# T3 of the second phase's weights formed once and kept in HBM, its splits placed behind evictions, and another order of loads, evictions and normalizations in a Winograd kernel

## The chip, the cores and the metric

The kernel runs on one core of one Trainium2 chip. The metric is device time in microseconds (us) of one execution. Engines go by their names in the profile: PE (TensorE, matmuls), PEld (its weight loads), DVE (VectorE), ACT (ScalarE), POOL (GpSimd), SP (SyncE, here only the queue that issues most transfers). Each engine works through its own instructions in order; a DMA issue is an instruction too, and holds up what stands behind it on the engine that issues it.

## The reference, cut to what matters

With `DEPTH = 1` only the pooling layer runs. `x` is 4096 tokens by 1024 channels, all float32.

```python
normed = rms_norm(x, norm_w[0])
u, gate = jnp.split(normed @ in_w, 2, axis=-1)          # in_w: 1024 x 2048
ug = u.reshape(b, s, 4, 256)
pooled = stack([trailing_mean(ug[:, :, g], (2, 4, 8, 16)[g]) for g in range(4)]) - ug
mixed = einsum('bsgc,gcd->bsgd', pooled, group_w) + group_b
y = mixed.reshape(b, s, 1024) * scale * silu(gate)
h = x + y @ out_w                                        # out_w: 1024 x 1024
return rms_norm(h, final_norm_w)
```

Pooling is linear along the tokens, so the kernel multiplies `group_w` into the u columns of `in_w` first ("folding") and pools afterwards.

## The kernel before, in words

**Products.** The big matrix products are done by the Winograd scheme: seven products P1 to P7 of half-size blocks for eight. One operand block is split in four quarters 11, 12, 21, 22; the weights too. For the weights of the input projection, 11 and 21 are the upper and lower rows of a gate half of `in_w`, times `norm_w` (`norm_c`), and 12 and 22 are folded u weights. The products use the weights 11 (P1), 21 (P2), T2 = 11 + T3 (P6), T3 = 22 - 12 (P7), T1 = 22 - T2 (P5), T4 = 21 - T2 (P4) and 22 (P3).

**Precision.** Each factor is split in a rounded high part (a copy on ACT into fp32r, L151, or L218 with a scale) and the rest (a subtraction on DVE, L145, or L219), and a product is three matmuls: high by high, high by low, low by high (`mm3`, L529). A product of the input projection is 48 matmuls of 128x128x512 (`product_in`, L538).

**Steps.** `steps` (L851) is the order of the work: 28 steps "a" (four blocks of 1024 tokens, each P1, P2, P6, P7, P5, P4, P3, the first half of the columns), then 28 steps "b" (the second half, "the second phase"), then 56 steps "o" (output projection). They are numbered from 0 here, so step 5 is P4 of the first block, 7, 14 and 21 are P1 of the blocks after it, and step 30 is P6 of the first block of phase two. A step needs both parts of two operand tiles `op` (four tiles in a ring, two for each step) and both parts of its weight tiles `w`. P1 and P2 add up in banks 0 to 3: before P2 starts there, ACT copies P1's sums to banks 4 to 7 (L151 `bank<-bank`, in `evict_in`, L639).

**The main loop** (L1074) issues for step n: loads for step n + 3 or so; squares of the next block's rows (ACT, L381), from which the factors 1/rms come (ACT sqrt L196, DVE reciprocal L200, POOL L197 to L206) and go by HBM (`rd`) to all partitions; the normalization of the operands of step n + 2 (`form`, DVE L148), then the splits of step n + 1 (`split_step`); pooling; the matmuls and evictions of step n (`run`); and late in "a", `make_wb` (L275), which makes the weights of phase two one step at a time, from loads that `load_wb` (L256) issued a step before. A scheduler then orders each engine's instructions by its own estimates; `issue_after` pins one behind another.

**Weights of phase two.** `make_wb` forms T3 from wvd pieces "12" and "22" (folded, kept in HBM) twice, for P6 and again for P7, for each of two halves h of the rows; P5's weights are formed as 11 - 12 and split with the sign turned (`split_negative`, L160).

**The opening** (L914 to L1014) folds in eight chunks (`fold`, L343: matmuls L348, evictions L359 on DVE or L363 on ACT), loads the rows of the first block (L374) and the gate rows `g0` and `g1` (L212), squares the rows, spreads 1/rms over the partitions with two matmuls (`spread_rs`, L398: `hl` on ACT and POOL, L407 on DVE, L415 on PE, then a copy on ACT), and makes the first operands and weights. Tiles come from the slot pools `st`, `vt`, `early` and `early5`, first freed first taken.

Of the kernel before, what the change touches and what calls it, by code (L numbers as in the profile page):

```python
# [60 lines left out]
def kernel(  # L61
# [82 lines left out]
    def sub(dst, a, b):  # L144
        return nc.vector.tensor_tensor(out=dst, in0=a, in1=b, op=ALU.subtract)  # L145
# [11 lines left out]

    latest_split = [None]

    def split_negative(dst, src):  # L160
        nc.scalar.activation(dst[:, 0], src, AF.Copy, scale=-1.0)
        nc.vector.scalar_tensor_tensor(
            out=dst[:, 1], in0=src, scalar=-1.0, in1=dst[:, 0].bitcast(F32),
            op0=ALU.mult, op1=ALU.subtract,
        )
# [6 lines left out]
    tails = const.tile([P, 2, 2, HIST], F32, name="tails")  # L172

    wvd = [dram.tile([P, 2, H], F32, name=f"wvd{k}") for k in range(4)]
    wod = {
        i: [dram.tile([P, 2, H], F32, name=f"wod{i}_{h}") for h in range(2)]
        for i in range(P1, P7 + 1)
# [63 lines left out]
    def pair(cs, h, kh):  # L241
        k = 4 * kh + 2 * h
        return cs[k : k + 2]
# [24 lines left out]
    def scaled(u, cs, other, op):  # L268

# [2 lines left out]
                out=u[:, j], in0=u[:, j], scalar=cs[j], in1=other[:, j], op0=ALU.mult, op1=op  # L272
            )

    def make_wb(i):  # L275

        for h in range(2):
            p = parts.pop((i, h))
            top, bottom = pair(norm_c, h, 0), pair(norm_c, h, 1)
            if i == P1:  # L280
                split_scaled(w[i][h], p["11"], top)
            elif i == P2:
                split_scaled(w[i][h], p["21"], bottom)
            elif i == P6:
                sub(p["12"], p["22"], p["12"])
                scaled(p["11"], top, p["12"], ALU.add)
                t2[h] = p.pop("11")
                split(w[i][h], t2[h])
            elif i == P7:
                sub(p["22"], p["22"], p["12"])  # L290
                split(w[i][h], p["22"])
            elif i == P5:
                scaled(p["11"], top, p["12"], ALU.subtract)
                split_negative(w[i][h], p["11"])
            elif i == P4:
                scaled(p["21"], bottom, t2[h], ALU.subtract)
                split(w[i][h], p["21"])
                give(t2.pop(h))
            else:
                split(w[i][h], p["22"])  # L300
            for u in p.values():
                give(u)

    def make_wo(h):
# [35 lines left out]
            )  # L340
        return r

    def fold(q, k, g, r, ps2, pool=None, on_vector=()):  # L343
# [12 lines left out]
        o = take(pool=pool)  # L356
        for kk in range(2):
            if kk in on_vector:
                nc.vector.tensor_scalar(  # L359
                    out=o[:, kk], in0=ps2[kk], scalar1=norm_c[k + kk], scalar2=None, op0=ALU.mult  # L360
                )
            else:
                nc.scalar.activation(o[:, kk], ps2[kk], AF.Copy, scale=norm_c[k + kk])  # L363
        return o
# [587 lines left out]
                g0.append(load_rows(in_w, 2 * hh, D))  # L952
    give(gw[0])
    load(1)
    g1 = [load_rows(in_w, 4 + 2 * h, D) for h in range(2)]
    for j in range(4):
        load_row(0, 1, j, early if j < 3 else None)
    load(2)

    def second_side(h):  # L960
# [7 lines left out]
        split(w[P6][h], g0[h])  # L968

    for n, (h, k) in enumerate(chunks):  # L970
        o = fold(1, k, gw[1], ru[1, k], banks[2 * (n % 2) : 2 * (n % 2) + 2], early5, (0,))
        stores.append((wvd[k // 2], o))
        if n == 0:
            for hh in range(2):
# [8 lines left out]
    second_side(1)  # L983
    form(1)
    split_step(1)
    for h in range(2):
        split_scaled(w[P2][h], g1[h], pair(norm_c, h, 1))
    for j in range(4):
        square_row(0, 1, j)
    with tc.high_priority():  # L990
        rs = stats(0, 1)

    def spread_second():
        with tc.high_priority():
# [79 lines left out]
    for n in range(2, len(steps)):  # L1074
# [108 lines left out]
```

## Time and profile before

| | us |
|---|---|
| median of 3 runs (967.61 to 970.01) | 967.83 |
| the execution that was profiled | 966.88 |
| its span, first to last instruction | 965.1 |
| PE busy | 950.2 (98%) |
| DVE busy | 733.4 (76%) |
| ACT busy | 451.7 (47%) |
| granted TensorE clock | 0.999 |

Busy time of PE is made of matmuls that overlap, with modelled ends: a run of matmuls is read by its start, its count and its length. Where a line says that PE was idle and names a releaser, the wait ended with that instruction.

### The profile page before, as it was taken

The page shows a single profiled execution, that of the slowest core. Times are in us where ns is not written, and L with a number is a line of the kernel's source. Part 1 is how long each engine was busy: PE and PEld are TensorE (multiplying, and loading weights), DVE is VectorE, ACT ScalarE, POOL GpSimd, SP SyncE. Part 2 cuts the span into 40 slices and gives each one's busy share as a digit, 9 for nine tenths or more (in the row PEclk, how much of TensorE's full clock was granted, in tenths as well). Part 3 has the DMA queues.
Part 4 walks back from the last instruction along what each step waited for, and adds up shares of the span by engine and source line. Part 5 has one row for each costly group of instructions (what it writes and reads, how often), then busy time and mean ns, then how long its engine had stood idle before and what let it go on. Part 6 is the DMA issues. An engine that isn't in the chain of part 4 may idle for free.

```text
span 965.1 us, 11084 instructions
## 1 busy us (share of the span) xinstructions
PE 950.2 (98%) x4184; PEld 784.7 (81%) x4184; DVE 733.4 (76%) x804; ACT 451.7 (47%) x679; POOL 49.3 (5%) x128
## 2 busy tenths in 40 slices
PE   9999999999999998999999999999999999999997
PEld 7777888888888887888888888888888888888885
DVE  2896993793796898596697599499977667577565
ACT  5868447347345455345444445553424424324333
POOL 0032100000000000000000000000101101001010
PEclk9999999999999999999999999999999999999999
DMA  9975865564556646015614733635646436356022
GB/s 341 380 285 158 307 218 180 210 237 138 204 209 223 240 162 236 7 44 210 247 44 153 259 128 119 235 135 194 239 154 217 149 136 220 113 191 213 27 88 88
DMA packets 67685, 177.01 MB, mean 183 GB/s; under 512 B 6704, under 2 KB 24240, under 8 KB 67632
## 3 DMA queue, kind: packets, MB, share of 16 engines
q1 hardware_dynamic: 61584, 156.11, 46.1%
q10 hardware_dynamic: 4320, 13.91, 3.6%
q0 software_dynamic: 1728, 6.29, 1.7%
q8 instruction: 33, 0.54, 0.2%
q14 instruction: 20, 0.16, 0.0%
HBM read 116.50 MB, written 59.78 MB: 183 GB/s over the span
## 4 chain that ended last, share of the span: by engine, by line
PE 76%; DVE 13%; DMA 6%; issue 2%; ACT 1%; POOL 1%; SPq 0%; ACTq 0%; DVEq 0%; POOLq 0%
PE bank L532 76%; DVE op L145 2%; DVE st L148 2%; DVE w L145 2%; DVE vt L142 2%; DMA rd<-rs 1%; DMA st<-in_x 1%; DMA st<-in_in_w 1%; DMA st<-rd 1%; DVE w L219 1%; DVE st L145 1%; DMA vt<-rd 1%; DMA vt<-sd 1%; DVE st L621 1%; DVE vt L145 1%
## 5 line engine op out<-in xcount | busy, mean ns | idle before, releaser
L532 PE MATMUL bank<-op,w 128*128 128x512 f32 x2688 | 612.2, 390 | 5.6 <-DVE op L145 5.0
L532 PEld LDWEIGHTS bank<-op,w 128*128 128x128 f32 x2688 | 503.7, 188 | 113.3 <-DVE op L145 7.1
L532 PE MATMUL bank<-w,op 128*128 128x512 f32 (+1 forms) x1356 | 305.0, 387 | 0.0
L532 PEld LDWEIGHTS bank<-w,op 128*128 128x128 f32 x1356 | 253.0, 188 | 52.0
L151 ACT ACTIVATE op<-st 128x1024 fp32r<-128x1024 f32 x119 | 125.6, 1056 | 146.8 <-PE bank L532 136.4
L145 DVE TENSOR_TENSOR op<-st,op 128x1024 fp32r<-128x1024 f32 x119 | 144.4, 1219 | 49.5 <-ACT op L151 49.2
L151 ACT ACTIVATE op<-vt 128x1024 fp32r<-128x1024 f32 x47 | 49.7, 1058 | 87.4 <-PE bank L532 83.3
L142 DVE TENSOR_TENSOR vt<-vt 128x1024 f32<-128x1024 f32 (+6 forms) x72 | 87.9, 1230 | 0.2
L151 ACT ACTIVATE vt<-bank 128x512 f32<-128x512 f32 x94 | 54.8, 596 | 48.5 <-PE bank L532 42.9
L145 DVE TENSOR_TENSOR op<-vt,op 128x1024 fp32r<-128x1024 f32 x47 | 57.4, 1222 | 20.6 <-ACT op L151 20.6
L830 DVE TENSOR_TENSOR st<-bank,st 128x512 f32<-128x512 f32 x60 | 41.2, 688 | 41.8 <-PE bank L532 41.6
L145 DVE TENSOR_TENSOR st<-st,st 128x1024 f32<-128x1024 f32 x35 | 42.4, 1220 | 14.0 <-DMA st<-wvd 12.9
L197 POOL TENSOR_SCALAR oms<-oss 128x2 f32<-128x2 f32 x14 | 9.7, 690 | 641.5 <-ACT st L741 637.1
L151 ACT ACTIVATE bank<-bank 128x512 f32<-128x512 f32 x48 | 27.5, 578 | 27.7 <-PE bank L532 23.1
L148 DVE TENSOR_TENSOR st<-st,st 128x1024 f32<-128x1024 f32 (+1 forms) x19 | 21.7, 1163 | 21.6 <-DMA st<-rd 21.6
L830 DVE TENSOR_TENSOR vt<-bank,vt 128x512 f32<-128x512 f32 (+1 forms) x37 | 24.9, 674 | 16.4 <-PE bank L532 16.3
L151 ACT ACTIVATE w<-st 128x1024 fp32r<-128x1024 f32 x22 | 23.2, 1061 | 27.0 <-PE bank L532 15.4
L145 DVE TENSOR_TENSOR w<-st,w 128x1024 fp32r<-128x1024 f32 x22 | 26.5, 1221 | 11.9 <-ACT w L151 11.7
L142 DVE TENSOR_TENSOR vt<-bank,vt 128x512 f32<-128x512 f32 x48 | 31.7, 684 | 0.1
L616 DVE SCALAR_TENSOR_TENSOR vt<-vt,vt 128x1024 f32<-128x1024 f32 x24 | 29.3, 1220 | 0.1
L348 PE MATMUL bank<-early,early 128*128 128x256 f32 x128 | 29.1, 387 | 0.1
L348 PEld LDWEIGHTS bank<-early,early 128*128 128x128 f32 x128 | 24.9, 196 | 4.3 <-issue 0.8
(119 smaller groups left out, 512.5 us busy)
## 6 DMA issues: line engine op xcount, KB each, us to landing
st<-in_x SPq DMA_DIRECT2D x33, 512.0 KB, 4.6
st<-in_xt SPq DMA_DIRECT2D x25, 512.0 KB, 5.7
st<-sd SPq DMA_DIRECT2D x25, 512.0 KB, 5.6
vt<-in_x SPq DMA_DIRECT2D x24, 512.0 KB, 4.2
sd<-st ACTq DMA_DIRECT2D x19, 512.0 KB, 5.9
st<-yd SPq DMA_DIRECT2D x19, 512.0 KB, 3.9
yd<-st SPq DMA_DIRECT2D x17, 512.0 KB, 2.7
out<-st SPq DMA_DIRECT2D x17, 512.0 KB, 4.5
```

Of the source, the lines that this page charges most:

```text
L142: nc.vector.tensor_tensor(out=dst, in0=a, in1=b, op=ALU.add)
L145: return nc.vector.tensor_tensor(out=dst, in0=a, in1=b, op=ALU.subtract)
L148: nc.vector.tensor_tensor(out=dst, in0=a, in1=b, op=ALU.mult)
L151: return nc.scalar.activation(dst, src, func)
L197: nc.gpsimd.tensor_scalar(out=ms, in0=ss, scalar1=1.0 / D, scalar2=EPS, op0=ALU.mult, op1=ALU.add)
L219: nc.vector.scalar_tensor_tensor(out=dst[:, 1], in0=u, scalar=c, in1=dst[:, 0].bitcast(F32), op0=ALU.mult, op1=ALU.subtract,)
L348: latest[0] = nc.tensor.matmul(ps2[kk][:, j * 256 : (j + 1) * 256], r[:, kk, 2 * j + t, :], g[:, 2 * j + t, :], start=(t == 0), stop=(t == 1),
L532: latest[0] = nc.tensor.matmul(ps, a, b, start=start and n == 0, stop=stop and n == 2, skip_group_check=True).ins
L616: nc.vector.scalar_tensor_tensor(out=s[:, :, at : at + H], in0=s[:, :, at : at + H], scalar=1.0 / win, in1=v[:, :, HIST:], op0=ALU.mult, o ...
L621: nc.vector.scalar_tensor_tensor(out=sg[:, j], in0=s[:, j, at : at + H], scalar=bias_c[2 * grp + j], in1=sg[:, j], op0=ALU.add, op1=ALU.mult,)
L830: partial["added"] = nc.vector.tensor_tensor(out=u[:, c], in0=ps[j][:, c], in1=u[:, c], op=ALU.add).ins
```

## The change

1. `form` for steps whose operands n + 2 are P1 or P2 of phase one (the normalizations) comes behind the splits of step n + 1, pinned to the latest of them.
2. T3 is formed once, in `save_t3`, after P6 of the third block: four loads, two subtractions on DVE, two stores to `t3d`. P6 and P7 load it from there. P5 is formed as 22 - T2 and split in the plain way.
3. `make_wb` falls into `form_wb`, ahead of the step's matmuls in the program, and `split_wb`, behind its evictions.
4. In the opening, the four row loads of the second half go ahead of the two `g1` loads; the fold's DVE evictions are kept for two of four chunks only (the others go to ACT); the splits of `g1` come behind the squares and the statistics.

```diff
+    t3d = [dram.tile([P, 2, H], F32, name=f"t3d{h}") for h in range(2)]
...
     def load_wb(i):
-            if i in (P1, P6, P5):
+            if i in (P1, P6):
                 p["11"] = load_rows(in_w, 2 * h, D + H)
             if i in (P2, P4):
                 p["21"] = load_rows(in_w, 4 + 2 * h, D + H)
-            for name, k, used in (("12", h, (P6, P7, P5)), ("22", 2 + h, (P6, P7, P3))):
+            for name, place, used in (("t3", t3d[h], (P6, P7)), ("22", wvd[2 + h], (P5, P3))):
                 if i in used:
                     p[name] = take()
-                    nc.sync.dma_start(out=p[name], in_=wvd[k])
+                    nc.sync.dma_start(out=p[name], in_=place)
+
+    def save_t3():
+        for h in range(2):
+            us = []
+            for k in (h, 2 + h):
+                us.append(take())
+                nc.sync.dma_start(out=us[-1], in_=wvd[k])
+            with tc.issue_after(evicted[0]):
+                sub(us[0], us[1], us[0])
+            nc.sync.dma_start(out=t3d[h], in_=us[0])
+            for u in us:
+                give(u)
...
-    def make_wb(i):
+    def form_wb(i):
...
+            if i == P6:
+                scaled(p["11"], pair(norm_c, h, 0), p["t3"], ALU.add)
+                give(p.pop("t3"))
+                t2[h] = p["11"]
+            elif i == P5:
+                sub(p["22"], p["22"], t2[h])
+            elif i == P4:
+                scaled(p["21"], pair(norm_c, h, 1), t2[h], ALU.subtract)
+                give(t2.pop(h))
+    def split_wb(i):
...
-            elif i == P6:
-                sub(p["12"], p["22"], p["12"])
-                scaled(p["11"], top, p["12"], ALU.add)
-                t2[h] = p.pop("11")
-                split(w[i][h], t2[h])
-            elif i == P7:
-                sub(p["22"], p["22"], p["12"])
-                split(w[i][h], p["22"])
-            elif i == P5:
-                scaled(p["11"], top, p["12"], ALU.subtract)
-                split_negative(w[i][h], p["11"])
...
     load(1)
-    g1 = [load_rows(in_w, 4 + 2 * h, D) for h in range(2)]
     for j in range(4):
         load_row(0, 1, j, early if j < 3 else None)
+    g1 = [load_rows(in_w, 4 + 2 * h, D) for h in range(2)]
...
-        o = fold(1, k, gw[1], ru[1, k], banks[...], early5, (0,))
+        o = fold(1, k, gw[1], ru[1, k], banks[...], early5, n < 2)
...
-    for h in range(2):
-        split_scaled(w[P2][h], g1[h], pair(norm_c, h, 1))
     for j in range(4):
         square_row(0, 1, j)
     with tc.high_priority():
         rs = stats(0, 1)
+    for h in range(2):
+        split_scaled(w[P2][h], g1[h], pair(norm_c, h, 1))
...
-        if n > 2:
+        normal = kind == "a" and step(n + 2)[2] in (P1, P2)
+        if n > 2 and not normal:
             form(n + 2)
         advance("split", n, split_step, split_reach)
+        if normal:
+            with tc.issue_after(latest_split[0]):
+                form(n + 2)
...
-        run(n)
         since = n - (NB - 1) * len(ORDER_IN) - 2
         if 0 <= since < len(ORDER_IN):
+            form_wb(ORDER_IN[since])
+        run(n)
+        if kind == "a" and b == 2 and i == P6:
+            save_t3()
+        if 0 <= since < len(ORDER_IN):
             with tc.issue_after(evicted[0]):
-                make_wb(ORDER_IN[since])
+                split_wb(ORDER_IN[since])
```

More of the change, by code (lines that the diff above doesn't have):

```diff
@@ L158 @@
     latest_split = [None]
[L160 to L165, printed above, removed]
     colt = const.tile([P, 24], F32, name="colt")
@@ L273, in scaled @@
             )
[L275 removed]
+    def form_wb(i):
         for h in range(2):
[L278 to L279 removed]
+            p = parts[i, h]
+            if i == P6:
[9 more added lines that the diff above has]
+        for h in range(2):
+            (u,) = parts.pop((i, h)).values()
             if i == P1:
[L281 removed]
+                split_scaled(w[i][h], u, pair(norm_c, h, 0))
             elif i == P2:
[L283 to L301 removed]
+                split_scaled(w[i][h], u, pair(norm_c, h, 1))
+            else:
+                split(w[i][h], u)
+            if i != P6:
                 give(u)
@@ L341, in load_wut, with fold @@
         return r
-    def fold(q, k, g, r, ps2, pool=None, on_vector=()):
+    def fold(q, k, g, r, ps2, pool=None, on_vector=False):
         for kk in range(2):
@@ L357, in fold @@
         for kk in range(2):
-            if kk in on_vector:
+            if on_vector and kk == 0:
                 nc.vector.tensor_scalar(
@@ L970 @@
     for n, (h, k) in enumerate(chunks):
-        o = fold(1, k, gw[1], ru[1, k], banks[2 * (n % 2) : 2 * (n % 2) + 2], early5, (0,))
+        o = fold(1, k, gw[1], ru[1, k], banks[2 * (n % 2) : 2 * (n % 2) + 2], early5, n < 2)
         stores.append((wvd[k // 2], o))
@@ L991 @@
         rs = stats(0, 1)
+    for h in range(2):
+        split_scaled(w[P2][h], g1[h], pair(norm_c, h, 1))
     def spread_second():
```

## The prediction

> **What bounds the kernel now.** I read first who PE waited for, then PE in order of time: starts, counts, lengths, and in brackets the idle time ahead with its releaser. PE is the bound; what can be won is what it waits.
>
> ```profile
> PE bank L532 <- DVE op L145: 5.0, 5, 2.5
> ```
>
> ```profile
> 34.24 0.58 PE L532 MATMUL bank<-op,w 128*128 128x512 f32 x1
> 35.35 13.08 PE L532 MATMUL bank<-op,w 128*128 128x512 f32 x56 [0.53 <-DVE early L359]
> 49.04 0.50 PE L415 MATMUL bank<-w,w 128*128 128x512 f32 x1 [0.61 <-DVE w L407]
> ...
> 50.16 41.61 PE L532 MATMUL bank<-op,w 128*128 128x512 f32 x182
> 93.68 22.06 PE L532 MATMUL bank<-op,w 128*128 128x512 f32 x96 [1.91 <-DVE op L145]
> 116.04 11.17 PE L532 MATMUL bank<-op,w 128*128 128x512 f32 x48 [0.31 <-DVE op L145]
> 127.39 2.79 PE L532 MATMUL bank<-op,w 128*128 128x512 f32 x11 [0.18 <-DVE op L145]
> ```
>
> ```profile
> 129.80 64.53 PE L532 MATMUL bank<-op,w 128*128 128x512 f32 x284
> 194.49 173.17 PE L532 MATMUL bank<-op,w 128*128 128x512 f32 x762 [0.15 <-DVE op L145]
> 370.15 282.95 PE L532 MATMUL bank<-op,w 128*128 128x512 f32 x1247 [2.49 <-DVE op L145]
> ```
>
> Spacing: 762 matmuls in 173.17, 0.227 each, so a step of 48 takes 10.9. The last of a run lasts some 0.39 though its successor was due after 0.227, so a wait loses its idle time plus 0.16; the lone matmul at 34.24 gives 1.11 - 0.23. Losses: A at 35.35 0.88; B at 49.04 0.77; C at 93.68 (step 5) 2.07; D at 116.04 (step 7) 0.47; E at 127.39 (step 8) 0.34; F at 194.49 (step 14) 0.31; G at 370.15 (step 30) 2.65. Sum 7.5: no more can be won, since the matmuls stay, all 4184 of them, and the end is not touched.
>
> **Blocks 1 and 2 (C, D, E, F): normalizations behind splits.** Here are DVE, then ACT, around step 5.
>
> ```profile
> 81.18 2.35 DVE L145 TENSOR_TENSOR w<-vt,w 128x1024 fp32r<-128x1024 f32 x2
> 91.26 1.22 DVE L148 TENSOR_TENSOR st<-st,vt 128x1024 f32<-128x1024 f32 x1 [7.73 <-DMA vt<-rd]
> 92.40 2.35 DVE L145 TENSOR_TENSOR op<-st,op 128x1024 fp32r<-128x1024 f32 x2
> ...
> 101.68 1.22 DVE L145 TENSOR_TENSOR op<-vt,op 128x1024 fp32r<-128x1024 f32 x1
> ...
> 126.12 2.35 DVE L145 TENSOR_TENSOR op<-st,op 128x1024 fp32r<-128x1024 f32 x2
> ```
>
> ```profile
> 85.73 2.01 ACT L151 ACTIVATE op<-st 128x1024 fp32r<-128x1024 f32 x2
> ...
> 92.50 1.06 ACT L381 ACTIVATE st<-st 128x1024 f32<-128x1024 f32 x1 [2.87 <-DMA st<-in_x]
> ...
> 95.95 1.05 ACT L151 ACTIVATE op<-vt 128x1024 fp32r<-128x1024 f32 x1
> ```
>
> ACT has step 5's high parts by 87.7, DVE is free at 83.5, yet step 5's low parts start at 92.40: the normalization of block 1 stands ahead of them and waits until 91.26 for 1/rms. In the changed order the low parts, two weight splits, step 5's four bank additions, a reciprocal and step 6's two low parts come first. They are done by 89, so C goes: 2.07.
>
> What is late next? The low parts of step 6 cannot move up by as much: ACT reaches their second high part at 95.95 to 97.0 behind squares of rows that land at 92.5. DVE then ends them at 98.5, and the two normalizations, which used the idle time before, end at 98.5 + 2 x 1.14 = 100.8, against 102.9 for the same work (101.68 + 1.22). From there to step 8's first low part DVE is always busy, with the same instructions: 127.3 (126.12 + 1.22) becomes 125.2. Step 7's low parts, now ahead of four normalizations, end near 112, before their due 113.4, so D goes. But step 8 is due at 127.05 - 2.07 - 0.47 = 124.5, and waits to 125.3. So E grows from 0.34 to 0.8, and C, D and E together give 2.1, between 1.0 (rows that land later) and 2.9 (E gone). As DVE sets step 8's start, a delay up to 0.8 in the opening costs nothing more here.
>
> F goes (0.3): step 14's second low part was behind three normalizations, and comes some 2 us earlier. Steps 15 and 22 get their normalizations later; counting DVE's new order at 1.14 for each, 1.33 for a pair of half-width ones and 0.6 for a bank addition, their low parts still end 1.7 and 1.9 ahead of need. If that cover fails, each pays its lateness.
>
> **Phase two (G).** DVE again, with the wait for the T3 parts:
>
> ```profile
> 317.00 1.23 DVE L145 TENSOR_TENSOR st<-st,st 128x1024 f32<-128x1024 f32 x1 [4.74 <-DMA st<-wvd]
> ...
> 331.45 1.22 DVE L145 TENSOR_TENSOR st<-st,st 128x1024 f32<-128x1024 f32 x1
> ...
> 354.01 2.35 DVE L162 SCALAR_TENSOR_TENSOR w<-st,w 128x1024 fp32r<-128x1024 f32 x2
> ...
> 366.60 2.36 DVE L145 TENSOR_TENSOR w<-st,w 128x1024 fp32r<-128x1024 f32 x2
> 368.87 2.36 DVE L145 TENSOR_TENSOR op<-st,op 128x1024 fp32r<-128x1024 f32 x2
> ```
>
> Step 30 starts when its first low part ends (368.87 + 1.2); from 317 on DVE hardly rests. Four subtractions for T3 go (4 x 1.14 = 4.5), two of them behind waits for several loads of which one is left. P5's four scaled halves (4 x 0.66) become two subtractions (2 x 1.14): 0.4 less. Six transfers of 512 KB leave the window. That is 4.9 us of DVE work against G's 2.65, with all else 2.1 to 2.4 earlier because PE is. Row by row in the new order, at these prices and with PE's earlier bank times, the low part ends near 363, when PE is due at 365.1: G goes whole, with 2 to spare. Less if T3's reload stalls DVE: for the second half its load is queued behind the split that frees its slot (about 305), lands some 4.5 later, and holds step 26's low part to 312, due at 322.
>
> `save_t3` adds two subtractions (2.3) near 225 to 235. DVE idles there:
>
> ```profile
> 229.57 1.23 DVE L145 TENSOR_TENSOR op<-st,op 128x1024 fp32r<-128x1024 f32 x1 [6.72 <-ACT op L151]
> ```
>
> So they are hidden. On SP two stores wait for them, and behind these stand block 3's loads and its 1/rms; priced below.
>
> **The opening (A, B).** ACT, DVE and POOL before step 1:
>
> ```profile
> 29.93 2.19 ACT L151 ACTIVATE op<-st 128x1024 fp32r<-128x1024 f32 x2 [1.21 <-DVE st L148]
> ...
> 35.63 0.67 ACT L363 ACTIVATE early<-bank,colt 128x512 f32<-128x512 f32 x1
> 36.20 1.94 ACT L218 ACTIVATE w<-vt,colt 128x512 fp32r<-128x512 f32 x3
> ...
> 42.35 1.04 ACT L381 ACTIVATE early<-early 128x1024 f32<-128x1024 f32 x1
> ...
> 45.47 0.57 ACT L151 ACTIVATE bank<-bank 128x512 f32<-128x512 f32 x1
> ...
> 48.06 0.20 ACT L151 ACTIVATE hl<-rs 128x4 fp32r<-128x4 f32 x1 [0.84 <-POOL rs L206]
> ```
>
> ```profile
> 34.55 1.41 DVE L359 TENSOR_SCALAR early<-bank,colt 128x512 f32<-128x512 f32 x2
> ...
> 41.73 1.22 DVE L145 TENSOR_TENSOR op<-st,op 128x1024 fp32r<-128x1024 f32 x1
> ...
> 46.65 0.17 DVE L200 RECIPROCAL rs<-tmp 128x4 f32<-128x4 f32 x1
> ```
>
> ```profile
> 46.98 0.20 POOL L201 TENSOR_TENSOR tmp<-rs,ms 128x4 f32<-128x4 f32 x1 [0.18 <-DVE vt L588]
> ...
> 80.30 1.02 POOL L201 TENSOR_TENSOR tmp<-rs,ms 128x4 f32<-128x4 f32 x1 [3.17 <-DVE rs L200]
> ```
>
> A goes: PE waited for a fold eviction on DVE that ACT now does at 31, long before 34.24. But step 1 (P2) now finds a new wait. In the changed order ACT does, from 29.93 to the second `hl`: four op copies and two w copies at 0.95, four fold evictions at 0.57, four squares at 1.04, three scaled g1 copies at 0.65 (1.94 for three), a square root of 0.2, and 0.3 of waiting: to 44.5. Only behind `hl` and the fourth scaled copy come the copies of P1's banks, which before began at 45.47, just in time; step 1 cannot start without the first.
>
> `hl` waits for the reciprocal. DVE ended step 1's low parts at 44.0 before (two at 1.14 from 41.73); without the two fold evictions of 34.55 (1.3 together) it ends them at 42.7. Then it takes the first low part of g1 behind its ACT copy (43.1) and the reciprocal at 43.8. From there to `hl` it took 1.41 before (46.65 to 48.06), with DVE at rest: 45.2. Here DVE has two more low parts of g1 to do; a POOL operation that met a busy DVE took 1.02 (80.30) instead of 0.20, so two that meet one add 0.8: `hl` at 46.0. I take that end, being nearer to the 80.30 row's situation. Then 0.1, the last scaled copy 0.65, the bank copy 0.57: PE starts step 1 at 47.4. It was due at 34.24 + 48 x 0.228 = 45.2, so the new wait loses 2.2 where A and B lost 1.65. The loads (512 KB in each place) swap places, squares' rows earlier, g1 later; ACT is too busy to notice, unless g1 lands after 42.4. The opening is 0.6 worse, between 1.65 better (no wait) and 1.5 worse.
>
> The Trainium skill, "SBUF — State Buffer", section "Who interferes with whom", says that a DVE instruction with two SBUF inputs contends with a GpSimd instruction that reads SBUF, and that the other one blocks fully. It speaks against this order, and the two POOL rows agree with it; by it the new wait is 2.2, without it 1.4, which is the sum's 0.8.
>
> **The sum.** Up to step 8 DVE decides, so the opening's 0.6 hides in E: 2.1 gained. With F 0.3 and G 2.65 that is 5.1. The profiled execution took 966.88 (span 965.1 and 1.8 around it), 0.95 under the median of the runs. From it comes 961.8, from the median of 967.83 comes 962.7; I forecast **962.6** for the median.
>
> **The rivals.**
>
> *The opening pays for the blocks* (0.12). If `hl` comes 1.5 to 2.5 later still, the opening loses up to 3 beyond now, and A to E give nothing. For: `hl` stands in front of the bank copies in ACT's order. Against: the squares' rows are loaded earlier. Left are F and G: 967.8 - 3.0 = 964.9 or a little above.
>
> *G stays, the edit doesn't do what it says* (0.10). Step 30's weights and loads are spread anew over slots; if a load lands late in front of DVE, as at 317.00 (4.74), the low part at step 30 waits as before. Then 2.4 is left: 965.4.
>
> *The opening is free* (0.12). If POOL is not held and rows land early, step 1 waits under 1 and E goes: 6.5 to 7.2 gained, 960.6 to 961.3.
>
> *Slower: SP behind T3's stores* (0.04).
>
> ```profile
> 221.46 9.69 SPq L460 DMA_DIRECT2D st<-in_xt  x2
> ...
> 238.45 1.37 SPq L460 DMA_DIRECT2D st<-in_xt  x2
> ```
>
> ```profile
> 260.25 1.22 DVE L145 TENSOR_TENSOR op<-st,op 128x1024 fp32r<-128x1024 f32 x1
> ```
>
> On SP the second store waits for a subtraction, that for a load into a slot which the first store must leave. At 4 to 5 each from 219 on, the second store is issued near 234. Behind it stand block 3's loads (second half at 238.45 before), whose operands were split from 260.25 on, due at 268. Nothing is lost up to some 242; each us after that is one of PE's. It decides against the change from 8 us later on, at 250: 5.1 gained, 8 lost, 970.7. Against: SP stood 9.69 there without harm.
>
> **How the numbers follow.** The forecast, gains of 3.5 to 6.4, has 0.62: 961.4 to 964.3. About 0.3%, 2.9 us, is what a measurement of this kernel can tell from no change, so faster means under 964.9. Faster: 0.62 and 0.12, 0.74. Same: 0.12 and 0.10, 0.22. Slower: 0.04. The range reaches down to half of the free opening, 960.6, and up over G's stay, 965.5.
>
> **What would show it.** C: no idle ahead of step 5; the low parts on DVE before the normalization. E: a wait near 125 at step 8, under 1. F and G: no wait at steps 14 and 30. The opening: no wait at 35, a wait of some 2 near 45 to 47 whose releaser is an ACT `bank<-bank` copy. T3: four subtractions `st<-st,st` fewer from 299 on, two more near 225 to 235. Wrong it would be by new waits from 371 to 655, where the slots turn over differently, or by step 1 starting after 48.5.

## The result

The changed kernel takes 961.88 us (median of 6 runs, 960.51 to 962.31) where the kernel before takes 967.93 (6 runs, 966.68 to 970.01): a ratio of 0.9931, with a 95% interval of 0.9917 to 0.9945. The forecast was 962.6. The execution that was profiled took 960.51, with a span of 958.7 (before 966.88 and 965.1), so the spans are 6.4 apart, the medians 6.05. PE is busy for 947.8 (99%), DVE for 729.2 (76%), ACT for 453.3 (47%).

PE's waits after the change, in us in total, number and longest one:

```profile
PE bank L536 <- ACT bank L151: 1.9, 1, 1.9
PE bank L921 <- DVE op L919: 1.5, 1, 1.5
PE bank L536 <- DVE op L145: 0.2, 1, 0.2
```

PE in order of time, after:

```profile
33.90 11.27 PE L536 MATMUL bank<-op,w 128*128 128x512 f32 x48
47.08 0.50 PE L536 MATMUL bank<-op,w 128*128 128x512 f32 x1 [1.92 <-ACT bank L151]
...
48.34 75.89 PE L536 MATMUL bank<-op,w 128*128 128x512 f32 x334
124.42 522.31 PE L536 MATMUL bank<-op,w 128*128 128x512 f32 x2303 [0.19 <-DVE op L145]
646.57 304.95 PE L536 MATMUL bank<-w,op 128*128 128x512 f32 x1356
```

The wait at L921 is the one with which PE starts, 1.49 us into the span; it stood there before too (L917). Of the seven waits of before that the prediction priced, one is left (step 8, 0.19 idle), and a new one stands at 47.08. Step 0 starts 0.34 earlier than before (33.90 for 34.24): the folding ran that much faster in this execution (over the 14 profiles step 0 starts from 33.51 to 34.58, with either opening). Step 8 starts 2.97 earlier (124.42 for 127.39), and the output projection 6.37 earlier (646.57 for 652.94). So 2.97 came up to step 8 and 3.40 behind it; the last stretch takes 304.95 in both.

DVE, then ACT, around steps 5 to 8 after the change:

```profile
78.27 0.17 DVE L194 RECIPROCAL rs<-tmp 128x4 f32<-128x4 f32 x1
...
85.02 2.36 DVE L145 TENSOR_TENSOR op<-st,op 128x1024 fp32r<-128x1024 f32 x2 [3.20 <-ACT op L151]
...
96.43 1.22 DVE L145 TENSOR_TENSOR op<-vt,op 128x1024 fp32r<-128x1024 f32 x1
97.57 2.35 DVE L148 TENSOR_TENSOR st<-st,vt 128x1024 f32<-128x1024 f32 x2
...
123.16 2.34 DVE L145 TENSOR_TENSOR op<-st,op 128x1024 fp32r<-128x1024 f32 x2
```

```profile
91.62 1.06 ACT L385 ACTIVATE st<-st 128x1024 f32<-128x1024 f32 x1 [3.80 <-DMA st<-in_x]
```

Step 5's low parts (85.02) now wait only for ACT's high parts, and the normalizations (97.57) stand behind step 6's low parts. The squares of block 1's rows start at 91.62; before it was 92.50. That 0.9 and the 1.7 at the reciprocal (78.27; the experiments give before's row) are what the prediction had not seen. Of the 1.7 only 0.9 reaches the rows, mostly because POOL's first operation behind this reciprocal took 3.29 us in this execution, where the same operation took 1.02 before (80.30 in the prediction):

```profile
78.59 3.29 POOL L195 TENSOR_TENSOR tmp<-rs,ms 128x4 f32<-128x4 f32 x1 [3.12 <-DVE rs L194]
```

The store of 1/rms was issued 4.48 after the reciprocal (82.75) where before it was 3.92.

Step 30's low parts after the change, on DVE:

```profile
359.49 2.35 DVE L145 TENSOR_TENSOR op<-vt,op 128x1024 fp32r<-128x1024 f32 x2
```

The first ends at 360.7. PE needs it 22 steps after step 8: 124.42 + 1056 x 0.2268 = 363.9, so 3 us are to spare where 2.65 were missing.

### The profile page after: what moved, and what is told of

The parts are those of the page before. It is cut to its first block, busy times and chain, and to the rows that moved or that the text cites. A ratio compares the mean times of both kernels' runs of the same rounds, so it can differ in the third digit from the quotient of the medians.

```text
span 958.7 us, 11087 instructions
## 1 busy us (share of the span) xinstructions
PE 947.8 (99%) x4184; PEld 785.6 (82%) x4184; DVE 729.2 (76%) x798; ACT 453.3 (47%) x681; POOL 47.8 (5%) x128
## 4 chain that ended last, share of the span: by engine, by line
PE 86%; DVE 6%; DMA 3%; ACT 3%; issue 1%; POOL 0%; SPq 0%; ACTq 0%; DVEq 0%; POOLq 0%
PE bank L536 86%; DMA st<-in_x 2%; DVE st L148 2%; DVE op L145 1%; DMA st<-in_in_w 1%; ACT early L385 1%; DMA early<-in_wut 1%; ACT w L151 0%; ACT op L151 0%; DVE st L145 0%; DVE w L213 0%; DVE st L142 0%; DVE w L145 0%; ACT st L385 0%; DVE vt L142 0%
## 5 line engine op out<-in xcount | busy, mean ns | idle before, releaser
L151 ACT ACTIVATE op<-st 128x1024 fp32r<-128x1024 f32 x126 | 132.9, 1058 | 181.1 <-PE bank L536 169.0
L145 DVE TENSOR_TENSOR op<-st,op 128x1024 fp32r<-128x1024 f32 x126 | 152.7, 1217 | 69.8 <-ACT op L151 69.6
L142 DVE TENSOR_TENSOR vt<-vt 128x1028 f32<-128x1028 f32 (+6 forms) x72 | 87.4, 1227 | 0.1
L151 ACT ACTIVATE vt<-bank 128x512 f32<-128x512 f32 x102 | 59.3, 595 | 46.6 <-PE bank L536 46.1
L151 ACT ACTIVATE op<-vt 128x1024 fp32r<-128x1024 f32 x40 | 42.4, 1060 | 70.9 <-PE bank L536 70.7
L145 DVE TENSOR_TENSOR st<-st,st 128x1024 f32<-128x1024 f32 x38 | 46.0, 1217 | 14.8 <-DMA st<-wvd 8.2
L145 DVE TENSOR_TENSOR op<-vt,op 128x1024 fp32r<-128x1024 f32 x40 | 48.7, 1220 | 10.0 <-ACT op L151 9.9
L142 DVE TENSOR_TENSOR vt<-bank,vt 128x512 f32<-128x512 f32 x54 | 35.6, 682 | 0.3 <-PE bank L536 0.2
L145 DVE TENSOR_TENSOR w<-st,w 128x1024 fp32r<-128x1024 f32 x20 | 24.2, 1220 | 11.9 <-ACT w L151 11.7
L625 DVE SCALAR_TENSOR_TENSOR vt<-vt,colt,vt 128x512 f32<-128x512 f32 x38 | 26.8, 743 | 0.0
```

The lines of the kernel that those rows point to most:

```text
L142: nc.vector.tensor_tensor(out=dst, in0=a, in1=b, op=ALU.add)
L151: return nc.scalar.activation(dst, src, func)
L625: nc.vector.scalar_tensor_tensor(out=sg[:, j], in0=s[:, j, at : at + H], scalar=bias_c[2 * grp + j], in1=sg[:, j], op0=ALU.add, op1=ALU.mult,)
```

## The experiments

The theory after this was: edit 1 gives steps 5, 7 and 14, edits 2 and 3 give step 30, edit 4 gives nothing. The rivals: step 30 has another cause that edit 1 also reaches, and edit 4 gives something through DVE. First, each edit alone and one more change to the opening. "Gain" below is the gain of a stage in the traces; ratios are to runs of the kernel before on the same chip, and are not the quotients of the medians.

### Edit 1 alone

```diff
+        normal = kind == "a" and step(n + 2)[2] in (P1, P2)
-        if n > 2:
+        if n > 2 and not normal:
             form(n + 2)
         advance("split", n, split_step, split_reach)
+        if normal:
+            with tc.issue_after(latest_split[0]):
+                form(n + 2)
```

> Before with edit 1 alone: the normalizations behind the splits; opening and T3 stay as before. Theory (DVE's low parts of steps 5, 7 and 14 only stood behind normalizations that waited for 1/rms): the waits at steps 5, 7 and 14 (2.07, 0.47 and 0.31 us lost) go, the wait at step 8 stays between 0 and 0.8, the waits of the opening (0.88 and 0.77) and of step 30 (2.65) stay. Gain 2.4 to 3.0 us in the span. Rival: part of the gain at step 5 came from the opening's other load order; then step 5 still waits for a low part, and the gain is under 1.5.

961.38 us (961.14 to 961.50), ratio 0.9935 [0.9921, 0.9949]: nearly all that the whole change gives; by their intervals the two can't be told apart. PE, from step 8 on:

```profile
125.31 522.31 PE L532 MATMUL bank<-op,w 128*128 128x512 f32 x2303 [0.68 <-DVE op L145]
647.46 304.95 PE L532 MATMUL bank<-w,op 128*128 128x512 f32 x1356
```

Steps 5, 7 and 14 wait no more, and the 0.84 lost at step 8 (0.68 + 0.16) and its start of 125.31 are what the prediction had worked out for the whole change (0.8 and 125.3). But step 30 waits no more either, with T3 formed twice. The theory falls in this half.

### Edits 2 and 3 alone

```diff
+    t3d = [dram.tile([P, 2, H], F32, name=f"t3d{h}") for h in range(2)]
+    def save_t3():
...
-    def make_wb(i):
+    def form_wb(i):
...
+    def split_wb(i):
...
```

The functions and their calls are those of the change's diff above.

> Before with edits 2 and 3 alone: T3 formed once and stored, weights formed ahead of the matmuls and split behind the evictions; opening and normalizations as before. Theory: nothing changes up to 200 us, the wait at step 30 (2.65) goes: gain 2.65. Rival: step 30's low part came earlier only because the earlier edits gave DVE slack; then a wait of 0.5 or more stays at step 30, and the gain is under 2.

964.90 us, ratio 0.9973 [0.9964, 0.9983]. The wait at step 30 is gone, the one at step 5 is there (1.84 idle). So either of two separate edits takes the same 2.65 away. What the two stores do to SP, seen on DVE and SP of this kernel:

```profile
247.81 1.23 DVE L148 TENSOR_TENSOR st<-st,st 128x1024 f32<-128x1024 f32 x1 [9.45 <-DMA st<-rd]
```

```profile
237.19 0.32 SPq L271 DMA_DIRECT2D t3d<-st  x1
...
239.29 0.32 SPq L398 DMA_DIRECT2D rd<-rs  x1
```

Block 3's first 1/rms is held on DVE, where its reciprocal stands behind the second T3 subtraction (237.08 for 231.18), and then on SP behind the second T3 store. It is used at 247.81, where before it was 238.58: 9 us later, and step 21 doesn't wait. But that uses up all the cover that there is. Step 21's low part ends at 271.3, and PE gets there at 195.05 + 336 x 0.2268 = 271.3:

```profile
270.08 1.22 DVE L145 TENSOR_TENSOR op<-st,op 128x1024 fp32r<-128x1024 f32 x1
```

With the forms late as well (below) the first 1/rms is used at 248.47, and step 21 waits 0.24 (272.01). So the slower rival had its place right (and DVE beside SP), and here its price was close.

### Edit 4 alone

```diff
     load(1)
-    g1 = [load_rows(in_w, 4 + 2 * h, D) for h in range(2)]
     for j in range(4):
         load_row(0, 1, j, early if j < 3 else None)
+    g1 = [load_rows(in_w, 4 + 2 * h, D) for h in range(2)]
...
-        o = fold(..., early5, (0,))
+        o = fold(..., early5, n < 2)
...
-    for h in range(2):
-        split_scaled(w[P2][h], g1[h], pair(norm_c, h, 1))
     for j in range(4):
         square_row(0, 1, j)
     with tc.high_priority():
         rs = stats(0, 1)
+    for h in range(2):
+        split_scaled(w[P2][h], g1[h], pair(norm_c, h, 1))
```

> Before with edit 4 alone: the opening's other order. Theory: the waits at 35 and 49 (0.88 and 0.77) go, one of about 2.2 comes ahead of step 1, behind an ACT copy of P1's banks; the waits of steps 5, 7 and 8 are behind a normalization whose 1/rms comes from rows that ACT squares, and these rows land by their own loads, so T(step 5 start) is set by DVE and hardly moves: between 0.3 slower and 0.5 faster in the span. Rival: edit 4 gives what was unexplained (0.9 us earlier rows): then step 5 starts 0.6 to 0.9 earlier, the waits after it too, and the gain is 0.6 to 1.

965.67 us, ratio 0.9981 [0.9970, 0.9991]. The new wait at step 1 is there (1.94 idle), but step 5 starts at 92.01 with 0.29 idle ahead, 1.67 earlier than before, and step 8 at 125.73, 1.66 earlier. The rival holds, and by more than it asked. Step 30 still waits 2.50. Where the gain comes from shows on DVE, first in the kernel before, then with edit 4 alone:

```profile
51.15 1.23 DVE L148 TENSOR_TENSOR vt<-vt,st 128x1024 f32<-128x1024 f32 x1 [1.38 <-ACT st L151]
...
79.97 0.18 DVE L200 RECIPROCAL rs<-tmp 128x4 f32<-128x4 f32 x1
```

```profile
49.59 1.23 DVE L148 TENSOR_TENSOR vt<-vt,st 128x1024 f32<-128x1024 f32 x1 [1.39 <-ACT st L151]
...
78.36 0.17 DVE L200 RECIPROCAL rs<-tmp 128x4 f32<-128x4 f32 x1
...
89.59 1.23 DVE L148 TENSOR_TENSOR st<-st,vt 128x1024 f32<-128x1024 f32 x1 [7.67 <-DMA vt<-rd]
```

The normalizations at 51.15 wait for the opening's second 1/rms, spread from `hl` (48.06 before, 45.83 here). From them to 83 DVE does not rest; at the end of that stretch stands the reciprocal for block 1's 1/rms, and behind it SP's store and the loads of rows. With `hl` 2.2 earlier the stretch starts 1.56 earlier (PE's two matmuls that spread 1/rms now stand behind step 1's first matmul, which waits until 47.18), and the normalization ahead of step 5 comes 1.67 earlier (89.59 for 91.26). The 14 profiles bear the chain out: the stretch starts anywhere from 49.49 to 51.51, and the reciprocal follows 28.77 to 28.85 behind its start in every one. PE's own opening is no faster: its place at step 5 is the same within 0.1 (50.16 + 41.61 before, 48.47 + 43.25 here).

### After, with the opening's second 1/rms on DVE

```diff
-    def rsqrt(dst, tmp, ms, ss):
+    def rsqrt(dst, tmp, ms, ss, eng=None):
+        eng = eng or nc.gpsimd
...
-        nc.gpsimd.tensor_tensor(out=tmp, in0=dst, in1=ms, op=ALU.mult)
+        eng.tensor_tensor(out=tmp, in0=dst, in1=ms, op=ALU.mult)
...
-        rsqrt(rs, tmp, ms, sums[b, half])
+        rsqrt(rs, tmp, ms, sums[b, half], nc.vector if (b, half) == (0, 1) else None)
```

> After, with the four small operations that follow the square root of the opening's second 1/rms on DVE instead of POOL, so that no POOL instruction is held by DVE's low parts of g1. Theory: the wait ahead of step 1 shrinks from 2.2 to between 0.5 and 1.2. If DVE alone sets the start of step 8 (124.4 us), as predicted, the wait of step 8 grows by what is won, and the total stays within 0.4 us of after. Rival: the chain of 1/rms by which DVE is timed moves with PE too (its banks come free earlier); then about 1 to 1.5 us stay, and the time is near 960.5 where after has 961.9.

959.87 us (959.57 to 960.38), ratio 0.9920 [0.9906, 0.9934]. PE:

```profile
45.55 2.11 PE L537 MATMUL bank<-op,w 128*128 128x512 f32 x8 [0.23 <-ACT bank L151]
...
123.56 522.33 PE L537 MATMUL bank<-op,w 128*128 128x512 f32 x2303 [0.61 <-DVE op L145]
```

The wait at step 1 falls from 1.92 to 0.23, further than expected, and not because `hl` comes earlier (46.39 for 45.73), but because the scheduler now puts P1's bank copies (44.92) ahead of it on ACT. The wait at step 8 grows from 0.19 to 0.61. Step 8 still starts when DVE lets it, 0.86 earlier than after, since block 1's rows landed 0.86 earlier (squares at 90.76 for 91.62). DVE's long stretch did not move (it starts at 49.51 for 49.49, its reciprocal is at 78.29 for 78.27). What differs is POOL's operation behind that reciprocal, which this edit does not touch:

```profile
78.62 1.02 POOL L196 TENSOR_TENSOR tmp<-rs,ms 128x4 f32<-128x4 f32 x1 [3.13 <-DVE rs L195]
```

It took 1.02 where it took 3.29 after, and the store of 1/rms is issued 0.54 earlier (82.21). So the first theory holds, DVE sets step 8's start; that DVE came 0.86 earlier is not shown to be an effect of this edit, since one trace of each doesn't tell how often the 3.29 occurs. The medians differ by 2.0, the ratios by 0.11% (1.1 us), the spans by 0.8; the last section comes back to that.

### Edit 1 in block 1 alone, and in block 3 alone

```diff
-        normal = kind == "a" and step(n + 2)[2] in (P1, P2)
+        normal = n in (5, 6)
```

This is edit 1's line for block 1; for block 3 it reads `n in (19, 20)`.

> Before with the normalizations put behind the splits in the first block's steps 5 and 6 alone (those of block 1); blocks 2 and 3 keep theirs ahead. Theory now (edit 1 has two separate gains, the wait of step 5 in block 1 and, through block 3, the wait of step 30): steps 5 and 7 wait no more, step 8 starts near 125.3, the waits of steps 14 and 30 (0.3 and 2.65) stay. Gain 2.0 in the span. Rival: step 30's wait was caused by an opening or a block 1 that ran late; then it shrinks here too, by more than 1, and the gain is over 3.

> Before with the normalizations behind the splits in steps 19 and 20 alone (those of block 3). Theory: up to 194 us all is as before; then DVE no longer idles 5.3 us at 258 for block 3's second 1/rms, all its work up to step 30 comes earlier, and the wait at step 30 goes with T3 still formed twice: gain 2.65. Rival: step 30's wait needs DVE work to be taken out (T3 once) or PE's slots to turn over otherwise; then it stays over 1.5.

Block 1 alone: 966.07 us (five runs, 963.54 to 966.81), ratio 0.9968 [0.9952, 0.9985]; step 8 starts at 125.12, and step 30 waits 2.39. Block 3 alone: 964.05 us, ratio 0.9957 [0.9942, 0.9972]; PE waits 1.58 at step 5 and 0.29 at step 7, and not at all at step 30. At steps 5, 8 and 30 both are as expected: edit 1 is two gains, and step 30's hangs on what block 3's normalizations do 100 us earlier. Two things are not as expected. The wait at step 14 (0.15 before) is listed in neither, though block 2's normalizations stand ahead as before; nor is it with edit 4 alone. And with block 1 alone a wait of 0.30 is new in step 28 (344.85), and the span is only 0.5 shorter (964.6), which the last section takes up. DVE at block 3, in the kernel before, then with block 3's moved:

```profile
251.46 1.22 DVE L142 TENSOR_TENSOR vt<-vt 128x1024 f32<-128x1024 f32 x1
257.98 1.23 DVE L148 TENSOR_TENSOR st<-st,st 128x1024 f32<-128x1024 f32 x1 [5.30 <-DMA st<-rd]
...
260.25 1.22 DVE L145 TENSOR_TENSOR op<-st,op 128x1024 fp32r<-128x1024 f32 x1
```

```profile
249.56 2.35 DVE L148 TENSOR_TENSOR st<-st,st 128x1024 f32<-128x1024 f32 x2
251.83 1.22 DVE L142 TENSOR_TENSOR vt<-vt 128x1024 f32<-128x1024 f32 x1
253.03 1.22 DVE L148 TENSOR_TENSOR st<-st,st 128x1024 f32<-128x1024 f32 x1
...
257.11 1.22 DVE L145 TENSOR_TENSOR op<-st,op 128x1024 fp32r<-128x1024 f32 x1
```

Before, DVE idles 5.3 us for the second 1/rms of block 3 and then works without rest to 294. Behind that it rests three times for loads of T3's parts (4.9, 3.2 and 4.7), but these come late too: the T3 subtraction that stood at 317.00 before stands at 313.86 with block 3's moved. So DVE does not make up for it before step 30.

### The saves of block 3 a step later

Why is that 1/rms late? Its way through HBM took 5.7 us from issue of the store to issue of the load (248.88 and 254.58), the first one 2.45 (232.58 and 235.03), and ACT's four saves of the normalized operands (issued from 242.7 to 249.2) run beside the slow one. This kernel is before with only these saves moved. The second pair of them then stores tiles that a later subtraction has changed in place, so the second phase of block 3 works with other values in one operand; the transfers and instructions are the same.

```diff
+            if saved is not None and by_pool is None:
+                held_saves.append((saved[h], u))
-            if saved is not None:
+            elif saved is not None:
...
         run(n)
+        with tc.issue_after(evicted[0]):
+            for place, u in waiting_saves:
+                nc.scalar.dma_start(out=place, in_=u)
```

> Before, with one thing moved: the four saves of block 3's first operands to HBM (512 KB each, issued by ACT at 242.7 to 249.2 us) are issued a step later; normalizations, T3 and the opening stay as before, DVE's order too but for two swaps. Theory: these four transfers are what makes the second 1/rms of block 3 slow on its way through HBM (store issued at 248.9, landed 5.3 later, where the first took 2.1); without them it lands 2 to 3 earlier, DVE's normalization starts at 255 to 256 where it was 258.0, and the wait at step 30 shrinks by as much: from 2.65 to between 0 and 0.6; gain 2 to 2.65. Rival: the way through HBM is slow for another reason (the order on SP, or the row loads); then the wait before the normalization stays within 1 of 5.3 and the wait at step 30 over 1.8.

965.11 us, ratio 0.9981 [0.9967, 0.9996]. SP, DVE (the normalization, then step 30's low parts) and PE of this kernel:

```profile
249.34 0.33 SPq L394 DMA_DIRECT2D rd<-rs  x1
251.92 0.33 SPq L427 DMA_DIRECT2D st<-rd  x1
```

```profile
255.09 1.23 DVE L148 TENSOR_TENSOR st<-st,st 128x1024 f32<-128x1024 f32 x1 [1.94 <-DMA st<-rd]
```

```profile
367.16 2.35 DVE L145 TENSOR_TENSOR op<-st,op 128x1024 fp32r<-128x1024 f32 x2
```

```profile
368.43 282.96 PE L536 MATMUL bank<-op,w 128*128 128x512 f32 x1247 [0.25 <-DVE op L145]
```

The way through HBM is down to 2.6, DVE's idle time from 5.30 to 1.94, and step 30's from 2.49 to 0.25. Of these last 2.24, 1.7 are DVE's (step 30's low part at 367.16 for 368.87); 0.5 are PE's, which comes that much later here because it lost more up to step 14 in this execution. Only the saves were moved, so for 1.7 of G's 2.65 the cause is shown: four 512 KB saves that the early normalizations set off slow a 2 KB store on which DVE waits. Edit 1 takes it away by making the normalizations, and so the saves, later.

### Which of edits 2 and 3

Edits 2 and 3 alone once with T3 formed twice again, and once with the forms put back behind the evictions:

```diff
...
+            if i in (P6, P7):
+                sub(p["t3"], p["x"], p["t3"])
+                give(p.pop("x"))
...
-        if kind == "a" and b == 2 and i == P6:
-            save_t3()
```

```diff
-            form_wb(ORDER_IN[since])
         run(n)
...
             with tc.issue_after(evicted[0]):
+                form_wb(ORDER_IN[since])
                 split_wb(ORDER_IN[since])
```

> The run of edits 2 and 3 alone, with T3 formed twice from the folded parts again (four loads and four subtractions more in phase two, no save of T3), the rest of the edits kept: forms ahead of the matmuls, splits behind the evictions, P5 as 22 - T2. Normalizations and opening as before. Theory: what edit 2 gives at step 30 is DVE work and loads taken out of the stretch from 299 to 370; with T3 formed twice 3 of the 4.9 us are back, and so is a wait at step 30 of 1 to 2.65; gain 0 to 1.6. Rival: the parting of forms and splits (edit 3) gives it; then no wait at step 30, gain 2.65.

> The run of edits 2 and 3 alone, with forms and splits both behind the evictions again (edit 3 undone, edit 2 kept: T3 formed once and stored). Theory: T3 once is what takes the wait away; no wait at step 30, gain 2.65, as with edits 2 and 3. Rival: without the parting the forms wait behind evictions, their slots come free later, and a wait of over 1 comes back at step 30.

964.58 us, ratio 0.9974 [0.9965, 0.9984], and 965.07 us, ratio 0.9978 [0.9967, 0.9988]: the wait at step 30 is absent in both. The first is not what its theory said. With T3 twice DVE still has the low part ready in time: it ends at 367.2, and PE gets there at 368.1. It starts 2.9 earlier than before (365.96). Of these, 1.1 is one weight split that now stands behind it. Of the rest, 1.3 is there by 354: ahead of that P5's weights are formed in the new way, and a wait of 1.1 for a load is gone. P5's new form is in both kernels and was not run alone. So T3 once is enough with it, and the parting is enough with it; what it brings by itself is not shown. Step 30 lacked 2.65 us, and edit 1 (in block 3) brings it without any of them.

### More on DVE, and less

The kernel with 1/rms on DVE, with the four small operations of block 1's first 1/rms there as well; and the same without edits 2 and 3.

```diff
-        rsqrt(..., nc.vector if (b, half) == (0, 1) else None)
+        rsqrt(..., nc.vector if (b, half) in ((0, 1), (1, 0)) else None)
```

> The kernel of the run with the opening's second 1/rms on DVE (959.87), with the four small operations of block 1's first 1/rms (at 78 to 82 us) on DVE too. Theory: what sets step 8's start is DVE, and what sets DVE there is a chain POOL, SP's queue, the load of two rows, ACT's squares: with the operations on DVE the store of 1/rms is issued some 3 us earlier (near 79.5, was 82.2), the two row loads behind it on SP as well, the rows land near 88 (were 90.8), the low parts of step 6 come 2 to 3 earlier, and the wait at step 8 (0.77 lost) goes: 0.8 faster, near 959.1. Rival: DVE is just as busy (the normalizations only lose idle time ahead of them, and the low parts of step 8 stay at 123.6): no change, 959.9.

> Edits 1 and 4 with both 1/rms chains on DVE (the opening's second and block 1's first), and T3 formed twice as before: edits 2 and 3 undone in the fastest kernel so far (959.11). Theory: once block 3's normalizations stand behind the splits, step 30 has no wait and edits 2 and 3 have nothing left to give: the same time within 0.5 us, no wait at step 30. Rival: PE is some 2.5 us earlier here than in the run of edit 1 alone, where step 30's first low part ended some 4 us ahead of need, and DVE has 2.2 us more to do from 299 on than with T3 stored; then a wait of up to 1.5 comes back at step 30.

959.11 us (958.93 to 959.40), ratio 0.9908 [0.9892, 0.9924], the fastest kernel of this study, and 959.35 us (958.67 to 960.47), ratio 0.9921 [0.9909, 0.9933]. PE of the first, then PE of the second:

```profile
48.57 596.51 PE L537 MATMUL bank<-op,w 128*128 128x512 f32 x2630
644.92 304.95 PE L537 MATMUL bank<-w,op 128*128 128x512 f32 x1356
```

```profile
124.35 522.33 PE L533 MATMUL bank<-op,w 128*128 128x512 f32 x2303 [0.85 <-DVE op L145]
646.52 304.95 PE L533 MATMUL bank<-w,op 128*128 128x512 f32 x1356
```

In the first, PE never waits from 48.57 on. The time came out as expected, its reason only by half: the store of 1/rms was not 3 us earlier (82.45 for 82.21), because on DVE the small operations take turns with 1.2 us splits. What moved is one of the two row loads, which the scheduler now issues ahead of the load of 1/rms; the squares of the two rows start at 88.23 and 90.99, where they were at 90.76 and 92.04. In the second kernel, with the same order, the last row landed later (its squares start at 92.83) in the execution that was profiled, and step 8 waits 0.85 again; its runs spread by 1.8. There the load of 1/rms, which stands ahead of that row's load on SP, was issued 2.6 us behind the store (82.90 and 85.51), where the first kernel took 1.5 (82.45 and 83.97). So E hangs on a transfer that lands within 2 us of its need; why it came later in the second, these rows don't show. Step 30 waits in neither: with edit 1 in place, edits 2 and 3 give nothing that can be measured.

### One piece of edit 4

```diff
-    for h in range(2):
-        split_scaled(w[P2][h], g1[h], pair(norm_c, h, 1))
...
         rs = stats(0, 1)
+    for h in range(2):
+        split_scaled(w[P2][h], g1[h], pair(norm_c, h, 1))
```

> Before with one piece of edit 4: the splits of g1 behind the squares and the statistics in the program (loads and fold evictions as before; the scheduler then moves only the last of the four splits behind the squares on ACT, and one behind the reciprocal on DVE). Theory: what edit 4 gives is an earlier second 1/rms of the opening (hl at 48.06 in before, 45.83 with all of edit 4), because DVE's normalizations behind it start a stretch in which DVE never rests until 83.5, and step 5's wait hangs on that stretch's end. So step 5 starts earlier here by as much as hl comes earlier, about 0.7 to 1.2, whatever the first waits of PE do. Rival: step 5's start follows the rows' loads, which this kernel leaves as they are; then step 5 starts within 0.3 of before's 93.7.

967.10 us, ratio 0.9996 [0.9986, 1.0006]. `hl` comes 0.62 earlier (47.44) and step 5 0.55 earlier (93.13), but 0.33 of both is a faster folding in this execution. Counted from step 0's start, step 5 comes after 59.2 us, and in the six other profiles with the old opening and block 1's old normalizations after 59.2 to 59.6; with all of edit 4 after 58.0. So this piece alone gives little or nothing that can be told from the folding. What it moves, it moves along the chain that was read above: the stretch 0.62 (50.53), the reciprocal 0.66 (79.31), the squares 0.56 (91.94).

## Why the prediction was right or wrong, point by point

- **C and D** went, as worked out: the low parts only stood behind normalizations that waited for 1/rms. F went too, but it is small (0.31), and no wait is listed at step 14 in three kernels that leave block 2's normalizations ahead, so that edit 1's part there took it is not shown.
- **A, B and the new wait.** PE waits ahead of step 1 until 47.08 (predicted 47.4) for ACT's copy of P1's first bank, and loses 47.08 - 33.90 - 48 x 0.228 = 2.2, as predicted. `hl` is at 45.73, and the POOL rows carry the 0.8 that was taken for a busy DVE. POOL and DVE after:

```profile
43.85 0.62 POOL L195 TENSOR_TENSOR tmp<-rs,ms 128x4 f32<-128x4 f32 x1 [1.35 <-DVE rs L194]
44.55 0.58 POOL L196 TENSOR_TENSOR tmp<-tmp,rs 128x4 f32<-128x4 f32 x1
45.22 0.19 POOL L197 TENSOR_SCALAR tmp<-tmp 128x4 f32<-128x4 f32 x1
45.50 0.20 POOL L200 TENSOR_TENSOR rs<-rs,tmp 128x4 f32<-128x4 f32 x1
```

```profile
43.66 1.42 DVE L213 SCALAR_TENSOR_TENSOR w<-vt,colt,w 128x512 fp32r<-128x512 f32 x2
```

  The two that meet DVE's splits end as a split ends (44.37 and 45.08, give or take 0.1), the two after them take 0.2. The rule of the Trainium skill that was weighed there holds in these rows. What the wait costs hangs on ACT's order: with the bank copies ahead of `hl` it shrank to 0.23.
- **"As DVE sets step 8's start, a delay up to 0.8 in the opening costs nothing more"** was true of PE and wrong of the edit. This is the step that failed: edit 4 was priced by what PE waits in the opening (0.6 worse, hidden), and by that alone. It also brings the second 1/rms 2.3 earlier, and with it a stretch of DVE that runs without rest to 83, block 1's 1/rms, the row loads behind it on SP, and ACT's squares (91.62; the prediction held them at 92.5). The term C, D, E, predicted at 2.1, is 2.08 with edit 1 alone and 2.97 with edit 4 added; 0.34 of that is the faster folding, the luck of this execution, and POOL's 3.29 us held the rows back by some 0.6. E, sized at 0.8, is 0.84 with the old opening and 0.35 with the new one.
- **G** went whole. The reason given is enough for it, but is not the only one, nor the first. The prediction read DVE from 317 on, found it busy, and counted 4.9 us of work out of that stretch. The work does go, and edits 2 and 3 alone are enough, even with T3's four subtractions put back; but the stretch is late for the most part because of 5.3 idle us at 258, behind a transfer, and edit 1 takes those away first. Two edits were credited with one gain each, C to F and G, where edit 1 alone takes all of them but E. The sum came out right because a wait can be removed only once.
- **T3's stores**: the second is issued at 233.72 (predicted 234), and step 21 doesn't wait. In the kernel with edits 2 and 3 alone the cover was seen at work: 9 us late and nothing lost, but with the second store at 237.19 and the old normalizations none of it was left; the prediction had put the edge at 242.
- **The sum.** 5.1 predicted and 6.05 measured by medians, 6.37 by spans: 0.9 of the difference is the opening's effect on DVE with the folding. About 0.4 more was won behind step 8 (3.40 measured, F and G are 2.96). It lies inside the runs of before, whose matmuls stand a little further apart (762 in 173.17 are 0.2270 each, 2303 in 522.31 are 0.2267); what spaces them no row shows.

## What to carry to other kernels

A wait on the bounding engine can be the end of a stretch in which another engine runs without rest: follow that stretch back to its first idle time, and price an edit by what it does there, even if it lies 100 us earlier. When several edits are meant for several waits, run each alone; gains that add up to more than the whole (here 0.65, 0.27 and 0.19% for 0.69%) tell that one wait was counted twice. A small transfer on which an engine waits is best kept out of the way of bulk stores that the same step sets off.

## What the runs showed of the hardware that was not expected

**PE's clock after a wait.** The kernel with edit 1 in block 1 alone won 2.27 up to step 8, and its span only 0.5. The view of stretches around its wait at step 30 (us, PE busy, granted clock, DMA share, GB/s) shows why:

```profile
368.00:369.00 1.00, 1.00 (x4) 0.83 0.72 213
369.00:370.00 1.00, 1.00 (x4) 0.50 0.80 303
370.00:371.00 1.00, 1.00 (x3) 0.50 0.45 180
371.00:372.00 1.00, 1.00 (x4) 0.50 0.00 0
372.00:373.00 1.00, 1.00 (x6) 0.97 0.00 0
```

```profile
367.97 284.56 PE L532 MATMUL bank<-op,w 128*128 128x512 f32 x1247 [2.39 <-DVE op L145]
```

Right behind the wait of 2.39 us the granted clock is at half for over 3 us, and the 1247 matmuls take 284.56 where before they took 282.95: 1.6 lost beside the wait itself. In the 14 profiles PE waits 1.84 to 2.50 us eleven times past the folding, and four times (here, and behind step 5's wait in the kernels of edits 2 and 3, of the late saves and of the late forms) such a dip follows; behind shorter waits none does. The Trainium skill, "TensorE: Matmul & The Clock Gate", section "Part 1: The HAM clock gate (the "warmup" mystery)", puts the half clock after at least one idle window of about 3.4 us; here the dip follows waits of 1.84 to 2.39 us, in some executions and not in others. This may be why the kernels without a wait of that size also spread less (958.93 to 959.40 and 961.14 to 961.50, against 965.76 to 970.11 for before), and why the kernel after, with 1.92 left at step 1, lies 2.0 over the kernel with 1/rms on DVE by medians but 0.8 by spans. The mean granted clock of the runs points the same way: in the kernel after it is 0.998 in the runs of 960.51 and 961.12 us and 0.996 in the four from 961.85 to 962.31; with edit 1 in block 1 alone it is 0.998 in the runs of 963.54 and 963.60 and 0.997 in the three from 966.07 to 966.81 (a dip of 3.3 us to half is 0.0017 of the mean). Where in these runs the clock fell, only a profile would show.

**A 2 KB store beside bulk stores.** The way of block 3's second 1/rms through HBM takes 2.5 to 2.6 us from issue to issue where the saves are later (edit 1 alone, its block 3 part alone, the late saves), 5.7 before, with four 512 KB saves beside it, and 4.1 in the kernel after (244.62 to 248.73), where only other loads are. Block 1's first 1/rms takes 1.5 before (83.89 to 85.35). The Trainium skill, "DMA: Bandwidth & Descriptors", section "Latency and other measured facts", has the access to HBM at 0.2 us on average and 2 under load, as the larger part of a transfer's fixed cost; the direction agrees, the 3 us more that are seen here exceed it.
